# A planner's prices in a two-block network kernel: more fixed time per instruction, half the column price for VectorE's scalar products

## The chip, the cores and the metric

The kernel is one program on one core of a Trainium2 chip. Its time is device time in microseconds (us) from launch to end; three runs stand at 4161.4, 4173.2 and 4182.5, and the median, 4173.2 us, is the time before. Lower is better. Engines are named as the profile names them: PE (TensorE's matmuls), PEld (its weight loads), DVE (VectorE), ACT (ScalarE), POOL (GpSimd), SP (SyncE, which issues most DMAs).

## What is computed

The reference is a float32 network of two blocks over 512 latent and 256 context tokens with 1024 features. The first block normalises, projects, runs three branches (a pooled mixer, a differential attention and a two-way recurrence), merges them and adds a mixture of 32 experts. The second has two layers: long convolutions and a gated recurrence (mLSTM) side by side, then latent attention, each with a convolutional feed-forward. What matters here, cut:

```python
def wkv_step(S, inp):                       # the first block's recurrence, per token
    r, w, k, v, a, b = inp
    sa = jnp.einsum('dbhvk,dbhk->dbhv', S, a)
    S = S * w[..., None, :] + sa[..., None] * b[..., None, :] + v[..., None] * k[..., None, :]
    return S, jnp.einsum('dbhvk,dbhk->dbhv', S, r)

def first_block(x, c, ctx, ...):
    mod = (s_lat @ w_ada[l] + b_ada[l]).reshape(B, N_MOD, 1, D)
    p_l = modulate(x, norm1_g[l], mod[:, 0], mod[:, 1]) @ w_in[l]
    ...                                     # att_l: attention; rwo_l: the recurrence
    mix_l = merge_branches((pool_mixer(pool_l, ...), att_l, rwo_l), gate_l, w_br[l], w_out[l])
    x = x + mod[:, 2] * mix_l
    x = x + mod[:, 5] * hier_moe(f_l, *moe_par)

def second_block(x, c, ctx, ...):           # for both layers
    sh1, sc1, g1, sh2, sc2, g2 = ada_mod(c[:, None, :], ada_w[layer], ada_b[layer])
    x_lat = x_lat + g1 * y_lat              # hyena_mlstm_mixer, then mla_mixer
    x_lat = x_lat + g2 * conv_ffn(...)
    return rmsnorm(x_lat, final_norm)
```

## The kernel before

Matrices are split into two parts, high (`h`) and low (`l`), and multiplied in three passes; the split is a copy on ACT and a subtraction on DVE. Three stretches of the program are woven from streams. Each stream is a Python generator that emits instructions and yields the moment at which its next matmuls could start. `weave` takes in turns the stream of the lowest rank that PE need not wait for.

- **First weave** (57 to 738 us of the profiled execution): inputs of the recurrence (`rwkv_inputs`, weights `ww`), attention (`wa`, then `S`, `P`, `pt`), the pooled mixer and the gates (`wo`, `wg`; the only stream of rank 2), and `rwkv_blocks`, which inverts blocks row by row on DVE (`blt`, `inv`). For each of four pairs of heads, the matmuls `dg` give `blk`, which is transposed to `blkT`; 31 dependent pairs of `blt` and `inv` instructions and two transposes `blkO` follow. The last head's chain ends the weave.
- **Recurrence** (738 to 1310 us): 24 units (`rwkv_unit`: `tkp`, `m`, `pg`, `pT`, `pZ`, `pR`, `pf`) and 24 steps (`rwkv_step`: `pc`, `pw`, `py`), with two units under way and at most three ready. A unit ends with `Zl`. Beside them, at rank 2, 160 matmuls `ada` (modulations of later layers), which depend on weights from memory alone and fill what the others leave.
- **First layer of the second block** (about 2222 to 2860 us): projections (`gp<-h,wi`), the mLSTM's heads (`mw`, `mN`, `mtp`), then long convolutions (`hf`, `fk`, `gtp`, `gc`, `hy`), and 82 further `ada` at rank 2.

What "could start" and "need not wait" mean is decided by `Clock`, a rough account kept while the program is traced. Each instruction is priced at `FIXED[engine] + EACH[engine] * columns`, and placed on its engine's list at the first time at which its inputs are written and there is room; 150 ns (`HOP`) are added from engine to engine. No time of the account is in the program: its only product is the order in which the streams' instructions are emitted. `ready` and `used` hold when tiles are written and free, and `after`, `room` and `later` read them. With nothing ready, the stream that is ready first is taken. When few columns were emitted lately (`active() < LOW`), rank 2 goes first.

The built program's order on each engine follows this one closely, though the build moves single instructions past each other. The rows of order below are the built program's. All instructions that are counted in the account are issued by one helper, so the profile shows them under one line, 350; groups are told apart by tiles.

The merge, the experts, both feed-forwards and the latent attention are each emitted as a single stream.

Of the kernel before, what the change touches and what calls it, by code (L numbers as in the profile page):

```python
# [22 lines left out]
FT = mybir.dt.float32  # L23
# [7 lines left out]
NL, NCX = 512, 256          # latent and context tokens  # L31
NT = NL + NCX               # context first, then latent
NE, CAP = 32, 64            # experts, slots of an expert
NOV = 16                    # further blocks of CAP slots, for experts with more tokens
# [3 lines left out]
ORDER = [[0, 1, 2, 3, 4, 5], [1, 0, 5, 4, 3, 2]]       # tiles of 128 tokens, forwards and backwards  # L38
# [3 lines left out]
# ------------------------------------------------------------------ layouts of the inputs  # L42
def _cols(v):
    """A vector over features as columns of 128 partitions."""
    v = np.asarray(v).reshape(-1)
    return v.reshape(-1, 128).T


def _unit(W, tiles):
    """Columns (128 at a time) of W, as one unit [128, k, n]."""  # L50
    K = W.shape[0]
    w = np.concatenate([W[:, t * 128:(t + 1) * 128] for t in tiles], axis=1)
    return w.reshape(K // 128, 128, -1).transpose(1, 0, 2).reshape(-1)
# [52 lines left out]
# ------------------------------------------------------------------ constants of the shapes  # L106
def _constants():
# [6 lines left out]
    st = [(p[:, None] < p[None, :]) * 1.0, (p[:, None] > p[None, :]) * 1.0]       # [s, t]  # L114
# [3 lines left out]
    for i in range(5, 7):  # L118
        m = 1 << i
        odd = (p // m) % 2 == 1  # L120
        low = ((p[:, None] // m == p[None, :] // m + 1) & odd[:, None]) * 1.0     # [t, s]
        C[f"lv{i}"] = np.concatenate([low, low.T], axis=1)
# [4 lines left out]
    # rotary halves: row d of the product is -u2 or u1  # L127
# [10 lines left out]
    for d in range(2):  # L138
        C[f"neg{d}"] = (1.0 - inc[d]) * -1e30                                     # [s, t]
# [20 lines left out]
def _tables():  # L160
    """More constants of the shapes, read when they are used."""
# [33 lines left out]
def _layout(I):  # L195
    """What the program reads: relaid inputs, and constants of the shapes."""
# [17 lines left out]
    # experts: gate and up in halves of their rows, down in halves of its columns  # L214
# [38 lines left out]
class Clock:  # L253
    """A rough account of when each engine is free and each tile is written, kept while the
    program is traced: it orders streams of instructions that share the engines."""
    FIXED = dict(vector=65.0, scalar=100.0, gpsimd=120.0)
    EACH = dict(vector=1.04, scalar=0.83, gpsimd=2.2)
    HOP = 150.0                 # from one engine to the next
# [7 lines left out]
    def __call__(self, eng, op, a, k):  # L266
# [13 lines left out]
        else:  # L280
            each = self.EACH[eng]
            if eng == "gpsimd" and op in ("tensor_scalar", "memset"):
# [18 lines left out]
    def place(self, eng, t, cost):  # L301
        """The first time from t on at which the engine has room for it."""
# [20 lines left out]
    def place_pe(self, t, cost):  # L323
        """The tensor engine's clock is halved after a tick of too few columns."""
# [8 lines left out]
    def active(self):  # L333
        """Columns of the last tick's length."""
# [29 lines left out]
class Ring:  # L364
    """A pool whose tiles' buffers are accounted for."""
# [13 lines left out]
class Feed:  # L379
    """Weights of a stream, in order: read ahead, and split one part ahead."""  # L380
# [32 lines left out]
class Builder:  # L413
# [7 lines left out]
    # ---- small helpers  # L421
# [25 lines left out]
    def split(self, hi, lo, src):  # L447
        """src as two parts that fp32r carries exactly."""
# [3 lines left out]
    # ---- weights: one unit read and split  # L452
# [13 lines left out]
    def gemm_fm(self, HL, m, kc, segs, tag="g", first=True, last=True, outs=None):  # L466
        """Feature-major product for the m-th 128 columns of a unit: one psum tile per segment.
        segs: (hi, lo, t0, t1), hi and lo [128, kc, tokens]."""
# [7 lines left out]
    def gemm_k(self, outs, H, L, k, segs, a, z, k0=0):  # L476
        """One tile of the contraction, in three passes; k0: where the weights' first tile stands."""
# [7 lines left out]
    # ---- 1/sqrt of a small tile, by Newton's steps  # L485
# [13 lines left out]
    def bcast_cols(self, out, cols, ident=None):  # L499
        """out[:, j*128:...] = cols[:, j] as a row on every partition; cols [128, j]."""  # L500
# [4 lines left out]
    def rms_rows(self, chunks, T, D, pool, tag="s"):  # L505
        """1/sqrt(mean of squares + eps) over all features of feature-major chunks, on every
        partition: a psum tile [128, T]."""
# [25 lines left out]
    # ---- norms of the residuals: the squares follow the sums closely  # L533
    def residual(self):
        """The residual of the latent tokens, and room for its norms."""
# [4 lines left out]
    def square(self, x, n):  # L540
        """The n-th features of a residual have their final values."""
# [10 lines left out]
    def rows(self, Ts, tag="g"):  # L552
        """1/sqrt(mean of squares + eps) of residuals, on every partition: psum tiles."""
# [17 lines left out]
    def modulated(self, norm, l, lo, hi, low, parts, pool, tag="g"):  # L571
        """rmsnorm(x) * (g * (1 + scale)) + shift of residuals, in two parts, into [:, k, t0:t0+T].
        parts: (residual, t0)."""
# [14 lines left out]
    def into(out, steps):  # L588
        """Steps, and their result into a list."""
# [3 lines left out]
    def run(steps):  # L593
        """A stream on its own."""
# [6 lines left out]
    def inner_norm(self, xs, T, g, hi, lo, t0, pool):  # L601
        """rmsnorm(x) * g, in two parts, into [:, k, t0:t0+T]."""
# [6 lines left out]
    # ------------------------------------------------------------------ the program  # L609
    def build(self, stages=("mix", "moe", "l0", "l1")):  # L610
# [21 lines left out]
        if "mix" in stages:             # not before the recurrence's own loads  # L632
# [62 lines left out]
    def gain(self, g, scale, name):  # L695
        """g * (1 + scale), as columns."""
# [4 lines left out]
    # ------------------------------------------------------------------ first block, mixer  # L701
# [2201 lines left out]
```

## Time and profile before

| | us |
|---|---|
| median of three runs | 4173.2 |
| span of the profiled execution | 4168.2 |
| PE busy in it | 3767.0 (90%) |
| DVE busy | 2573.4 (62%) |
| ACT busy | 1679.6 (40%) |
| first weave, 57 to 738 us | 681 |
| recurrence, 738 to 1310 us | 572 |
| first layer of block two, 2222 to 2860 us | 638 |

Read first how busy each engine is in each of the three stretches, and the granted clock of TensorE there (1 is 2.4 GHz, 0.5 is 1.2 GHz). A busy PE includes overlapped starts of matmuls, and time at the lower clock. Then look inside: who waits for whom, and where the filler `ada` stands.

### The profile page before, as it was taken

How to read it: one execution, taken by the hardware profiler on the slowest of the kernel's cores; microseconds unless marked ns; L12 is line 12 of the kernel's file. 1: busy time of each engine (PE TensorE's matmuls, PEld its weight loads, DVE VectorE, ACT ScalarE, POOL GpSimd, SP SyncE). 2: the span in 40 equal slices, each digit the busy share in tenths (PEclk: the TensorE clock that was granted, in tenths of full speed). 3: DMA queues.
4: the chain of work that ended last, by engine and by line, in shares of the span. 5: the costliest groups of instructions: out<-in, count | busy, mean ns of one | idle time of the engine just before them, and what ended most of it. 6: DMA issues, size and time to landing. Idle time of an engine off the chain costs nothing.

```text
span 4168.2 us, 52257 instructions
## 1 busy us (share of the span) xinstructions
PE 3767.0 (90%) x18404; PEld 2830.7 (68%) x18404; DVE 2573.4 (62%) x4611; ACT 1679.6 (40%) x2869; POOL 987.3 (24%) x1066
## 2 busy tenths in 40 slices
PE   8988998799997977888888999898999998999998
PEld 4776665466565755555554887577888886667886
DVE  4587989576665488899984466545333325545444
ACT  3322443333332366666663454223322324434342
POOL 0222211322220367777770000010100100000010
PEclk9989998899987989999999999999999999999999
DMA  4223323534325478888874232421221221012332
GB/s 186 92 75 124 110 70 106 157 121 147 116 80 176 129 246 290 294 298 289 294 242 153 96 124 98 151 74 46 66 64 58 68 64 50 14 40 72 101 96 86
DMA packets 240124, 537.95 MB, mean 129 GB/s; under 512 B 44274, under 2 KB 66451, under 8 KB 237940
## 3 DMA queue, kind: packets, MB, share of 16 engines
q1 hardware_dynamic: 199312, 461.64, 33.4%
q10 hardware_dynamic: 36708, 61.39, 4.2%
q0 software_dynamic: 3840, 11.54, 0.9%
q8 instruction: 148, 2.42, 0.2%
q14 instruction: 116, 0.95, 0.1%
HBM read 486.24 MB, written 48.24 MB: 128 GB/s over the span
## 4 chain that ended last, share of the span: by engine, by line
PE 51%; DVE 9%; DMA 6%; POOL 5%; issue 4%; ACT 3%; SPq 0%; another core or an unknown queue 0%; POOLq 0%; ACTq 0%; DVEq 0%
PE gp L350 32%; DMA ew<-w_exp 3%; POOL el L350 3%; PE ada L350 3%; DVE el L350 2%; PE S L350 2%; PE vp L350 1%; PE eg L350 1%; PE o L350 1%; ACT eh L350 1%; PE fk L350 1%; PE ed L350 1%; PE m L350 1%; PE pc L350 1%; DMA wada<-ada_w 1%
## 5 line engine op out<-in xcount | busy, mean ns | idle before, releaser
L350 POOL TENSOR_TENSOR el<-ew,eh 128x256 fp32r<-128x256 f32 (+1 forms) x384 | 479.7, 1271 | 196.7 <-ACT eh L350 188.8
L350 DVE TENSOR_TENSOR el<-ew,eh 128x768 fp32r<-128x768 f32 x379 | 458.0, 1234 | 58.9 <-ACT eh L350 57.8
L350 ACT CAST wh<-wr 128x512 fp32r<-128x512 f32 (+5 forms) x306 | 199.5, 675 | 600.7 <-PE gp L350 554.1
L350 PE MATMUL gp<-h_hi,wh 128*128 128x512 f32 (+1 forms) x1128 | 401.5, 359 | 6.6 <-ACT h_hi L350 3.8
L350 ACT CAST eh<-ew 128x1024 fp32r<-128x1024 f32 x384 | 381.2, 1048 | 16.4 <-PE ec L350 9.8
L350 PE MATMUL gp<-h_lo,wh 128*128 128x512 f32 (+1 forms) x1128 | 386.1, 357 | 0.7 <-DVE h_lo L350 0.3
L350 DVE TENSOR_TENSOR wl<-wr,wh 128x512 fp32r<-128x512 f32 (+5 forms) x306 | 228.1, 764 | 245.9 <-ACT wh L350 243.7
L350 PE MATMUL gp<-h_hi,wl 128*128 128x512 f32 (+1 forms) x1128 | 343.3, 356 | 0.0
L350 PE MATMUL ada<-wada,adas 128*24 128x512 f32 (+2 forms) x576 | 298.3, 641 | 20.7 <-DMA wada<-w_ada_a 9.9
L350 PE MATMUL eg<-el,xg 128*128 128x512 f32 x512 | 233.3, 457 | 90.0 <-POOL el L350 65.8
L350 POOL MEMSET cvb<- 128x1 f32 x170 | 9.6, 98 | 1068.0 <-DVE fg L350 691.4
L350 PEld LDWEIGHTS gp<-h_hi,wh 128*128 128x128 f32 x1128 | 211.9, 189 | 57.8 <-ACT h_hi L350 8.8
L350 PEld LDWEIGHTS gp<-h_lo,wh 128*128 128x128 f32 x1128 | 212.8, 189 | 34.8 <-DVE h_lo L350 3.2
L350 PE MATMUL eg<-eh,xg 128*128 128x512 f32 x512 | 217.0, 427 | 4.6 <-ACT eh L350 4.5
L350 PEld LDWEIGHTS eg<-el,xg 128*128 128x128 f32 x512 | 103.5, 202 | 168.0 <-POOL el L350 117.0
L350 PEld LDWEIGHTS gp<-h_hi,wl 128*128 128x128 f32 x1128 | 189.8, 190 | 16.7 <-DVE wl L350 0.3
L350 PE MATMUL gp<-z_hi,wh 128*128 128x512 f32 (+1 forms) x528 | 187.8, 356 | 0.0
L350 PE MATMUL gp<-z_lo,wh 128*128 128x512 f32 (+1 forms) x528 | 179.2, 354 | 0.0
L350 PE MATMUL gp<-z_hi,wl 128*128 128x512 f32 (+1 forms) x528 | 158.8, 355 | 0.0
L350 PEld LDWEIGHTS ada<-wada,adas 128*24 128x24 f32 (+2 forms) x576 | 47.1, 103 | 148.4 <-issue 114.1
L350 PE MATMUL gp<-h_lo,wih 128*128 128x256 f32 (+1 forms) x384 | 132.3, 345 | 0.0
L350 PE MATMUL gp<-h_hi,wih 128*128 128x256 f32 (+1 forms) x384 | 128.8, 356 | 0.0
(846 smaller groups left out, 9515.4 us busy)
## 6 DMA issues: line engine op xcount, KB each, us to landing
ew<-w_exp SPq DMA_DIRECT2D x384, 512.0 KB, 5.7
wada<-ada_w SPq DMA_DIRECT2D x192, 256.0 KB, 3.0
wr<-ffn_up SPq DMA_DIRECT2D x176, 256.0 KB, 2.7
wada<-w_ada_b SPq DMA_DIRECT2D x64, 256.0 KB, 3.0
wg<-w_in_a SPq DMA_DIRECT2D x48, 256.0 KB, 2.7
wi<-w_in SPq DMA_DIRECT2D x48, 256.0 KB, 2.6
wr<-ffn_dn SPq DMA_DIRECT2D x32, 384.0 KB, 3.1
wr<-ffn_dn SPq DMA_DIRECT2D x32, 320.0 KB, 3.3
```

The source lines that it names most:

```text
L350: return f(*a, **k)
```

## The change

Three prices of `Clock` grow, and one operation's price per column is halved. DVE's fixed price goes from 65 to 155 ns, ACT's from 100 to 180, POOL's from 120 to 200; the prices per column change little, except POOL's (2.2 to 2.6 ns). `tensor_scalar` on DVE (a tensor with one or two scalars, or a scalar per partition) counts half per column, as it did on POOL. The rest of the diff takes out comments and docstrings.

```diff
 class Clock:
...
-    FIXED = dict(vector=65.0, scalar=100.0, gpsimd=120.0)
-    EACH = dict(vector=1.04, scalar=0.83, gpsimd=2.2)
-    HOP = 150.0                 # from one engine to the next
+    FIXED = dict(vector=155.0, scalar=180.0, gpsimd=200.0)
+    EACH = dict(vector=1.05, scalar=0.85, gpsimd=2.6)
+    HOP = 150.0
     DMA = 2600.0
     TICK, ENOUGH = 10240 / 3, 3060
...
             each = self.EACH[eng]
-            if eng == "gpsimd" and op in ("tensor_scalar", "memset"):
+            if eng == "gpsimd" and op in ("tensor_scalar", "memset") or eng == "vector" and op == "tensor_scalar":
                 each /= 2
             cost = self.FIXED[eng] + each * n
```

The order of the built program changes in the three woven stretches alone. The number of matmuls stays 17,097 in all, with the same work in them. What is not the same in number is ACT's loads of its function tables, which the build puts where two neighbouring functions need different ones: 30 before, 26 now; the four fewer are in the first layer of block two.

**Recurrence, PE, in the last of the 24 units.** Before:

```order
L350 MATMUL pg<-TZ,Ah 128x128 x4
L350 MATMUL ada<-wada,adas 24x512 x2
L350 MATMUL pg<-TZ,Ah 128x128 x4
L350 MATMUL pT<-TZ,identr 128x512
L350 MATMUL pT<-G,TZ 128x128 x4
L350 MATMUL ada<-wada,adas 24x512
L350 MATMUL pT<-TZ,identr 128x512
L350 MATMUL pT<-G,TZ 128x128 x4
```

The change:

```order
L350 MATMUL py<-Us,Mh 128x128
L350 MATMUL py<-Us,Ml 128x128
L350 MATMUL pg<-TZ,Ah 128x128 x4
L350 MATMUL pT<-TZ,identr 128x512
L350 MATMUL pT<-G,TZ 128x128 x4
L350 MATMUL pZt<-const_58,T 128x128 x4
```

The same steps of a unit stand without `ada` between them: of the 160, the last now comes before the 19th unit is through, with 857 matmuls of the recurrence behind it, where it came with 32 behind it.

**Long convolutions, PE, between the short ones (256 tokens, `hy`) and the first filter of the long ones (`fk`).** Before:

```order
L350 MATMUL hf<-hw_22971,hh_22973 128x256 x4
L350 MATMUL ada<-wada,adas 24x512 x3
L350 MATMUL hf<-hw_22971,hh_22973 128x256 x2
L350 MATMUL ada<-wada,adas 24x512 x3
L350 MATMUL gtp<-const_58,hg 128x128 x4
L350 MATMUL ada<-wada,adas 24x512 x2
L350 MATMUL fk<-fch,dft5120h 128x256
L350 MATMUL fk<-fch,nyq 128x256
```

The change:

```order
L350 MATMUL hf<-hw_23002,hh_23004 128x256 x5
L350 MATMUL gtp<-const_58,hg 128x128 x4
L350 MATMUL fk<-fch,dft5120h 128x256
L350 MATMUL fk<-fch,nyq 128x256
L350 MATMUL gtp<-const_58,hg 128x128
```

Eight `ada` are gone from this place. Of the stretch's 82, the projections' part held 13 and now holds 22; behind the projections stood 53, now 39; ahead of them 16, now 21.

**First weave, DVE, in the last head's chain of `blt` and `inv`.** Before:

```order
L350 TENSOR_TENSOR blt<-inv,blkT 128x24x24
L350 TENSOR_TENSOR nm<-mx 128x1
L350 TENSOR_TENSOR wgl<-wg,wgh 128x512
L350 TENSOR_REDUCE inv<-blt 128x24
L350 TENSOR_SCALAR nm<-nm 128x1
L350 TENSOR_TENSOR wgl<-wg,wgh 128x512
L350 TENSOR_TENSOR blt<-inv,blkT 128x25x25
```

The change:

```order
L350 TENSOR_TENSOR blt<-inv,blkT 128x22x22
L350 TENSOR_REDUCE inv<-blt 128x22
L350 TENSOR_TENSOR blt<-inv,blkT 128x23x23
L350 TENSOR_REDUCE inv<-blt 128x23
L350 TENSOR_TENSOR blt<-inv,blkT 128x24x24
L350 TENSOR_REDUCE inv<-blt 128x24
L350 TENSOR_TENSOR blt<-inv,blkT 128x25x25
```

The attention's and the gates' instructions stand earlier, so this chain's end is alone. Counted in the built order: between the first and the fourth `blkT`, DVE had 749 instructions and now has 788; from the fourth to the last `blkO`, 111 and now 100. PE had 1428 matmuls between the last `dg` of the first head and that of the fourth, and now has 1565; behind that, to the weave's end, 203 and now 81.

## Rows read from the trace of the kernel before

**Rows 1.** The page's part 1: busy us, share of span, instructions.

```profile
PE 3767.0 (90%) x18404; PEld 2830.7 (68%) x18404; DVE 2573.4 (62%) x4611; ACT 1679.6 (40%) x2869; POOL 987.3 (24%) x1066
```

**Rows 2.** Windows of the three woven stretches: length, busy times, clock, DMA share.

```profile
core 0: us, PE busy (x) PEld busy (x) DVE busy (x) ACT busy (x) POOL busy (x), PEclk, DMA share, GB/s
...
57.00:738.00 681.00, 621.06 (x2800) 457.93 (x2800) 541.76 (x1092) 243.29 (x499) 118.25 (x133) 0.92 0.28 95
738.00:1310.00 572.00, 511.60 (x2927) 344.92 (x2927) 369.53 (x704) 199.67 (x390) 150.96 (x190) 0.89 0.38 116
...
2222.00:2860.00 638.00, 603.33 (x3297) 465.96 (x3296) 338.42 (x872) 233.29 (x462) 36.42 (x112) 0.95 0.32 106
```

**Rows 3.** Groups by form, whole span: busy us, mean ns of one, idle before.

```profile
L350 ACT ACT_TABLE_LOAD x30 | 38.5, 1283 | 8.6 <-DVE mx L350 3.6 <-issue 2.1 <-DVE mu L350 1.3
...
L350 DVE TENSOR_TENSOR G<-pg,const 128x512 fp32r<-128x512 f32 x48 | 32.7, 685 | 16.4 <-PE pg L350 16.2
...
L350 DVE TENSOR_SCALAR P<-P,sm 128x768 f32<-128x768 f32 x32 | 19.8, 618 | 0.7
```

**Rows 4.** Windows of the first weave, from one `blkT` to the next, and after.

```profile
244.00:392.00 148.00, 133.24 (x636) 104.63 (x635) 120.73 (x223) 42.89 (x77) 34.83 (x34) 0.91 0.29 98
392.00:530.00 138.00, 126.15 (x530) 85.73 (x529) 125.33 (x260) 53.03 (x121) 22.32 (x22) 0.94 0.32 106
530.00:670.00 140.00, 125.71 (x533) 84.62 (x531) 125.05 (x268) 54.80 (x125) 21.87 (x23) 0.94 0.30 99
670.00:738.00 68.00, 59.06 (x216) 39.12 (x216) 60.74 (x118) 21.50 (x51) 5.82 (x3) 0.90 0.25 80
```

**Rows 5.** The tile `blkT`: ns min/median/max, first and last start.

```profile
L350 DVE STREAM_TRANSPOSE blkT<-blk x4: 1234/1236/1248, 244.2 to 670.5; 128x1024 f32<-128x1024 f32 x4
```

**Rows 6.** Groups of PE in 57 to 738 us, with idle time before and releasers.

```profile
L350 PE MATMUL gp<-h1l_hi,wgh 128*128 128x512 f32 x192 | 86.2, 449 | 5.3 <-ACT gt L350 5.2
...
L350 PE MATMUL S<-kx,q 64*128 64x384 f32 x128 | 54.9, 543 | 7.6 <-ACT P L350 5.9 <-DMA kx<-at_k 1.6
...
L350 PE MATMUL dg<-AR,BK 64*128 64x128 f32 x96 | 16.8, 348 | 8.8 <-DVE BK L350 6.0 <-DVE blk L350 2.6 <-DVE nm L350 0.2
```

**Rows 7.** Windows of the recurrence; behind 1137 us start its last 853 other matmuls.

```profile
738.00:1137.00 399.00, 360.53 (x2010) 231.46 (x2011) 261.91 (x477) 142.40 (x276) 117.17 (x154) 0.90 0.43 136
1137.00:1310.00 173.00, 151.06 (x919) 113.46 (x918) 107.62 (x227) 57.27 (x114) 33.79 (x36) 0.86 0.24 71
```

**Rows 8.** The same windows, `ada` alone: PE, PEld, ACT (two PE records each matmul).

```profile
738.00:1137.00 399.00, 133.19 (x254) 19.73 (x254) 0.57 (x1) 0.90 0.43 136
1137.00:1310.00 173.00, 37.11 (x66) 5.04 (x66) 0.57 (x1) 0.86 0.24 71
```

**Rows 9.** Start and end of a unit (tiles `tkh`, `Zl`): first and last start.

```profile
L350 ACT CAST tkh<-tkp x24: 576/586/600, 751.9 to 1249.5; 128x512 fp32r<-128x512 f32 x24
...
L350 DVE TENSOR_TENSOR Zl<-Zt,Zh x24: 682/1240/3883, 794.3 to 1282.8; 128x512 fp32r<-128x512 f32 x24
```

**Rows 10.** Timeline of PE in the last unit: start, us, instruction.

```profile
1266.25 0.45 PE L350 MATMUL pT<-TZ,identr 128*128 128x512 f32 x1
1266.54 0.56 PE L350 MATMUL pT<-G,TZ 128*128 128x128 f32 x4
```

**Rows 11.** Windows of the projections, and of the convolutions with `ada` in them.

```profile
2290.00:2590.00 300.00, 297.11 (x1792) 253.93 (x1791) 181.98 (x554) 150.14 (x295) 4.03 (x64) 0.97 0.29 99
...
2685.00:2785.00 100.00, 94.58 (x490) 63.96 (x489) 46.41 (x92) 22.09 (x53) 19.32 (x28) 0.99 0.34 107
```

**Rows 12.** Timeline of PE around `gtp`; in brackets idle time and its releaser.

```profile
2725.89 0.63 PE L350 MATMUL gtp<-const,hg 128*128 128x128 f32 x4 [2.71 <-DMA hg<-hy_x]
2726.44 1.90 PE L350 MATMUL ada<-wada,adas 128*24 128x512 f32 x4
...
2801.51 0.63 PE L350 MATMUL gtp<-const,hg 128*128 128x128 f32 x4 [2.62 <-DMA hg<-hy_g]
2802.81 1.22 PE L350 MATMUL gc<-gt_hi,dft5120h 128*128 128x256 f32 x4 [0.68 <-ACT gt_hi L350]
```

## The prediction, made before the changed kernel was run

> **What bounds the kernel now.** The page's first part comes first: PE is busy for 90% of the span, DVE for 62%, ACT for 40% [rows 1]. That makes PE the engine whose gaps count on the whole, but the change touches three stretches alone, and the share is an average over all. So the windows of the three woven stretches come next [rows 2]. PE stands idle there for 681 − 621 = 60 us, 572 − 512 = 60 us and 638 − 603 = 35 us, at a mean granted clock of 0.92, 0.89 and 0.95. A perfect order could bring back no more than these 155 us and what the clock loses; a worse order can take more.
>
> The first weave is the one in which another engine is nearly as full. From the first `blkT` to the fourth, 426.3 us [rows 5], DVE is busy for 120.7 + 125.3 + 125.1 = 371.1 us (87%) and PE for 385.1 us (90%) [rows 4]. PE's waits in the whole weave that have a name are small and spread: 5.3 us before the gates, 7.6 before `S`, 8.8 before `dg` [rows 6]. DVE's row of dependent instructions is what the weave ends on, so the moment of the fourth `blkT` matters.
>
> In the recurrence a unit takes from its first cast `tkh` (751.9 first, 1249.5 last) to its `Zl` (794.3 first, 1282.8 last): 33.3 us for the last one, while 24 of them take 530.9 us, 22.1 us each [rows 9]. With two under way, 16.7 us each would be the floor of the dependent work. Of the filler, 127 `ada` stand in the first 399 us and 33 in the last 173 us [rows 8]; one costs PE 1.90 / 2 = 0.95 us [rows 12].
>
> In the first layer of block two, the projections fill PE for 297.1 of 300 us and the part of the convolutions that has `ada` for 94.6 of 100 us [rows 11]. That stretch leaves little to win.
>
> The new prices are nearer to what DVE does. A `G` of 512 columns now counts 155 + 1.05 x 512 = 693 ns, 597 before, and takes 685; a scalar product over 768 columns counts 155 + 0.525 x 768 = 558 ns, 864 before, and takes 618 [rows 3]. Better prices do not by themselves make a better order, since the weave only asks who is ready first and takes filler when nobody is. With dearer DVE and ACT instructions the account sees PE wait more often, and rank 2 is taken earlier. All the moves below have that shape: filler and side work come forward, and the ends of the stretches lose it.
>
> **The change part by part.** The account has no instruction in the program, so no matmul is added or removed, and the price is that of moves alone.
>
> *A, first weave.* DVE has 39 instructions more between the first and the fourth `blkT`. At the mean of that part, 371.1 us / 751 = 0.49 us, they are +19 us. Behind the fourth, DVE has 11 fewer, at 60.7 / 118 = 0.51 us each [rows 4]: −6 us, and if the waits in it (68.0 − 60.7 = 7 us) go too, since the chain is then alone, −13 us. With DVE as the pacemaker that is +6 to +13, of which I take +9. The ends: on PE, 137 more matmuls stand ahead of the fourth head's `dg`, mostly gates, at 385.1 us / 1428 = 0.27 us each, +37 us; less the 7 us at the end, +30. Downwards, if the earlier gates fill all the gaps, the 426.3 us shrink to DVE's own 371 + 19 = 390, −36 us, with −13 behind: −49. DVE's row is the nearest, because its 87% includes few waits that an order could cure, and the work that the end loses is work that the middle must do.
>
> *B, recurrence, first part.* 33 more `ada` come ahead: 33 x 0.95 = +31 us. PE's idle time there is 399 − 360.5 = 38.5 us [rows 7], of which the start until the first `tkh`, 14 us [rows 9], has nothing to fill it with. At the best the other 25 us take them: +6. At the worst they stand before ready work: +31. I take the middle, +18.
>
> *B, tail.* The last 857 matmuls, 173 us before, lose 33 `ada`: −31 us of PE. But the filler stood in holes. In the first part `ada` had 133.2 of 399 us (33%), in the tail 37.1 of 173 us (21%) [rows 8]; DVE's busy share was 261.9 / 399 = 66% and 107.6 / 173 = 62% [rows 7]. With a third less filler, the work on the other engines went no faster, so it is not the filler that holds it up. The place shows why: between `pg` and the `pT` that needs `G` now lies a single matmul, 0.29 us from its start to the next (1266.25 to 1266.54) [rows 10], against 685 ns for `G` [rows 3]; the `ada` taken away leave a wait of about their length. At the floor of 16.7 us a unit the tail's 173 / 22.1 = 7.8 units would take 131 us, −42; if every hole stays open, 0. I take −8. Together B is +18 − 8 = +10, with ends of +6 − 42 = −36 and +31.
>
> *C, first layer of block two.* Nine more `ada` in the projections, where PE has no gap [rows 11]: 9 x 0.95 = +9 us. Five more ahead of them: +5, of which about 2 paid. Behind, 14 fewer: −13, of which about 6 come back as waits: a `gtp` that waited 2.71 us with `ada` near it and one that waited 2.62 and left 0.68 more without [rows 12] show that the filler hides two or three us a time, in the two or three places that lose it. Sum: +9 + 2 − 13 + 6 = +4. The four table loads that go, 4 x 1.28 = 5 us of ACT [rows 3], lie on an engine that is busy for 233 of 638 us [rows 2], and I count −1 for them, with ends of 0 and −5. C is +3, with ends of −10 (the nine are hidden, the loads count) and +15 (the filler at the end was all cover).
>
> A rule speaks for C's lower end. PE's busy time says that the projections have 3 us to spare, while its weight loads are busy for 253.9 of 300 us, 85% [rows 11]. The Trainium skill ("Perfetto Trace Analysis", section Identifying the Most-Contended Engine) holds that busy time of matmuls is no good measure of headroom, since pipelined instructions look otherwise in a trace than what they cost, and that the share of weight loads is to be read. By it 46 us would be free in the projections, the nine `ada` would cost nothing there, C would be −6, and the total 4186. No row here shows an `ada` taken in for nothing beside `gp`.
>
> The sum is 9 + 10 + 3 = +22 us. The profiled execution's span is 4168.2 us, and 5.0 us lie around it to the median of 4173.2. So 4168.2 + 22 + 5.0 = 4195.
>
> **The rivals.**
>
> *Faster: the waits in the first weave are cured.* PE's waits behind ACT and DVE there were made by prices that were too low: 65 ns for a start that counts 155 now. If the earlier gates fill PE's 41 us of gaps between the first and the fourth `blkT` without holding up DVE, A is −40 instead of +9, and the rest stays: 4173 − 40 + 13 = 4146. For it speaks that the prices fit [rows 3]; against it, DVE at 87% must do 39 instructions more in that part. It decides if DVE's share there rises to 95%.
>
> *Slower: the recurrence's tail without filler loses the clock.* The granted clock was 0.86 in the tail with 33 `ada` in it, and 0.97 to 0.99 where PE never waited [rows 7, 11]. If half of the tail's remaining 151.1 − 37.1 = 114 us of PE falls to the lower of the two levels (1.2 GHz, a mean of 0.75), they take 114 x 0.86 / 0.75 = 131 us, +17 us in place of −8; with the first part at its upper end, +31, B is +48 and the total 4173 + 9 + 48 + 3 = 4233. Against it: the dependent chains may hide a slower PE. It decides if the granted clock behind the last `ada` is under 0.78.
>
> *Nothing: the change doesn't do what it says.* The same instructions stand on the same engines, the moves are local, and each gain at one end is paid at the other: A, B and C each within 5 us, 4173. For it: every `ada` that comes earlier does go away later. Against it: the tail's row on DVE's share.
>
> **How the numbers follow.** Something like the sum, 4183 to 4215: 0.41. Faster by the first weave, about 4146: 0.19. Slower by the tail, about 4233: 0.18. Nothing: 0.22. The forecast is 4195. The range runs from 4140, which takes in most of the faster case, to 4235, the slower one. A measurement of this kernel can tell about 0.5%, 21 us, from no change, and the sum lies on that edge. Slower by over that are the tail's 0.18 and over half of the forecast's, 0.24; faster the first weave's 0.19, less what falls within 21 us of it, 0.18 in all; the same what is left, 0.40.
>
> **What would show it right or wrong.** In the profile of the changed kernel the fourth `blkT` should start some 19 us later than 670.5 and the weave end some 9 us later than 738; the last `ada` of the recurrence should start before 1180, and the recurrence be 582 us long, with its last 165 us at DVE's old share and a clock below 0.86; the layer should be 641 us long, with the projections 9 us longer. A is wrong if the fourth `blkT` starts no later than before: then DVE was not the pacemaker. B's tail is wrong if its units come at less than 20 us each: then the filler did hold up the chains. C is wrong if the projections grow by less than 4 us with nine more `ada` in them. Any difference over 5 us outside the three stretches would mean that something but the order has changed.

## The result and the profile after

The changed kernel takes 4198.6 us in the median of 11 runs, against 4173.2 before: a ratio of 1.0066 with a 95% interval of 1.005 to 1.0081, slower by 25 us. The forecast was 4195. Its profiled execution has a span of 4196.4 us, 28.2 more than that of before.

The page's first part and the windows of the three stretches, moved to where they now lie (length, busy times, clock, DMA share; they answer to [rows 1] and [rows 2]):

```profile
PE 3780.8 (90%) x18404; PEld 2855.7 (68%) x18404; DVE 2571.2 (61%) x4611; ACT 1673.6 (40%) x2865; POOL 987.3 (24%) x1066
```

```profile
57.00:749.00 692.00, 613.70 (x2808) 453.51 (x2808) 544.16 (x1104) 244.34 (x500) 117.25 (x134) 0.93 0.28 94
749.00:1333.00 584.00, 533.46 (x2919) 374.65 (x2919) 366.07 (x692) 198.53 (x390) 152.34 (x189) 0.85 0.37 113
2250.00:2888.00 638.00, 599.77 (x3296) 464.21 (x3295) 338.34 (x870) 227.44 (x457) 36.31 (x112) 0.96 0.33 106
```

The first weave is 11 us longer, the recurrence 12, the layer the same; PE's busy time in the recurrence rose by 22 us at a clock of 0.85 instead of 0.89. To place it closer, these landmarks of both traces serve (start times in us):

| | before | after | difference |
|---|---|---|---|
| first weave, to the last `blkO` | 735.7 | 746.1 | +10.4 |
| recurrence, from there to the last `py` | 561.3 | 573.9 | +12.6 |
| merge and experts, to the last `cp` | 910.5 | 914.9 | +4.4 |
| first layer, to the last `hy` | 622.2 | 622.9 | +0.7 |
| the rest of the span | 1338.5 | 1338.5 | 0.0 |

The +4.4 lies where the two programs have the same order. In ten further kernels with that order this stretch takes 914 to 921 us, so the execution of before was a short one there. The three woven stretches account for +23.7.

**First weave.** From one `blkT` to the next and behind the last (as [rows 4]), the tile's own line (as [rows 5]) and PE's waits (as [rows 6]):

```profile
238.00:391.00 153.00, 140.18 (x695) 110.38 (x694) 124.83 (x238) 45.80 (x80) 31.45 (x31) 0.96 0.31 104
391.00:529.50 138.50, 130.38 (x563) 89.94 (x561) 128.63 (x274) 58.22 (x135) 24.68 (x26) 0.98 0.34 113
529.50:693.00 163.50, 145.82 (x596) 99.73 (x596) 132.44 (x279) 60.47 (x138) 23.11 (x23) 0.92 0.28 91
693.00:749.00 56.00, 25.04 (x86) 14.78 (x85) 50.83 (x102) 9.37 (x24) 2.46 (x3) 0.72 0.15 44
```

```profile
L350 DVE STREAM_TRANSPOSE blkT<-blk x4: 1235/1245/1246, 237.9 to 693.0; 128x1024 f32<-128x1024 f32 x4
```

```profile
L350 PE MATMUL gp<-h1l_hi,wgh 128*128 128x512 f32 x192 | 83.8, 436 | 0.3 <-ACT gt L350 0.2
...
L350 PE MATMUL S<-kx,q 64*128 64x384 f32 x128 | 52.0, 524 | 1.5 <-PE gp L350 0.5 <-ACT P L350 0.5 <-ACT pr L350 0.2
...
L350 PE MATMUL dg<-AR,BK 64*128 64x128 f32 x96 | 16.6, 343 | 8.6 <-DVE nm L350 4.7 <-DVE rsq_w L350 2.2 <-DVE blk L350 1.0
```

The fourth `blkT` starts at 693.0, 22.5 us later, and the stretch behind it is 12 us shorter, with DVE busy for 50.8 of 56 us and PE for 25.0 where it had 59.1. The named waits before the gates and `S` have gone from 5.3 and 7.6 us to 0.3 and 1.5, which won no time.

**Recurrence.** Its first part and its last 173 us (as [rows 7]; the last `ada` starts at 1150), with `ada` alone behind them (PE, PEld, ACT, as [rows 8]):

```profile
749.00:1150.00 401.00, 372.41 (x2047) 224.58 (x2047) 253.86 (x452) 140.82 (x274) 114.67 (x149) 0.96 0.49 153
1150.00:1323.00 173.00, 156.88 (x854) 146.27 (x853) 108.50 (x226) 56.30 (x114) 35.15 (x38) 0.63 0.08 24
```

```profile
749.00:1150.00 401.00, 159.36 (x320) 25.16 (x320) 0.58 (x1) 0.96 0.49 153
1150.00:1323.00 173.00, 0.41 (x1) 0.00 (x0) 0.57 (x1) 0.63 0.08 24
```

Without a single `ada` the last 173 us are as full as before, PE 156.9 against 151.1 us. The granted clock is 0.63 in place of 0.86, so most of the tail runs at the lower of the two levels, 1.2 GHz. The first part has all the filler and a clock of 0.96 in place of 0.90. DVE's work per us stayed: 108.5 of 173 us, 107.6 before.

**First layer.** The projections by their first matmul group (duration min/median/max in ns, first and last start), before and after; then the windows that answer to [rows 11]:

```profile
L350 PE MATMUL gp<-h_hi,wih x384: 274/390/795, 2293.6 to 2590.2; 128*128 128x256 f32 x192
```

```profile
L350 PE MATMUL gp<-h_hi,wih x384: 274/390/748, 2320.5 to 2622.3; 128*128 128x256 f32 x192
```

```profile
2318.00:2618.00 300.00, 297.39 (x1775) 247.78 (x1774) 175.36 (x522) 142.48 (x286) 4.06 (x64) 0.98 0.32 104
2716.00:2816.00 100.00, 87.49 (x491) 67.70 (x491) 51.12 (x105) 23.18 (x57) 21.65 (x30) 0.92 0.23 70
```

From the first to the last start of this group the projections take 301.8 us instead of 296.6, +5. The part ahead of them is 0.5 us shorter and the part behind 3.9, where PE is busy for 87.5 of 100 us, without `ada`, at a clock of 0.92 (94.6 at 0.99 before).

### The profile page after: what moved, and what is told of

Its sections match the earlier page's. It is cut to its first block, busy times and chain, and to the rows that moved or that the text cites. A ratio compares the mean times of both kernels' runs of the same rounds, so it can differ in the third digit from the quotient of the medians.

```text
span 4196.4 us, 52227 instructions
## 1 busy us (share of the span) xinstructions
PE 3780.8 (90%) x18404; PEld 2855.7 (68%) x18404; DVE 2571.2 (61%) x4611; ACT 1673.6 (40%) x2865; POOL 987.3 (24%) x1066
## 3 DMA queue, kind: packets, MB, share of 16 engines
q1 hardware_dynamic: 199312, 461.64, 33.3%
## 4 chain that ended last, share of the span: by engine, by line
PE 52%; DVE 8%; DMA 5%; POOL 5%; issue 5%; ACT 3%; SPq 0%; another core or an unknown queue 0%; POOLq 0%; ACTq 0%; DVEq 0%
PE gp L350 32%; POOL el L350 4%; PE ada L350 3%; DMA ew<-w_exp 3%; DVE el L350 2%; PE S L350 2%; PE eg L350 1%; PE vp L350 1%; PE o L350 1%; PE pc L350 1%; PE fk L350 1%; ACT eh L350 1%; PE m L350 1%; PE py L350 1%; PE ed L350 1%
## 5 line engine op out<-in xcount | busy, mean ns | idle before, releaser
L350 ACT CAST eh<-ew 128x1024 fp32r<-128x1024 f32 x384 | 381.1, 1048 | 16.3 <-PE ec L350 9.7
L350 PE MATMUL ada<-wada,adas 128*24 128x512 f32 (+2 forms) x576 | 284.9, 619 | 31.5 <-DMA wada<-ada_w 10.5
```

The lines of the kernel that those rows point to most:

```text
L350: return f(*a, **k)
```

## The experiments

Two questions were open: whether each stretch pays for its own new order, and by what; and whether the prices make the loss, or the one order that they happen to draw. All runs are collected here; the experiments follow. "To the tail" runs from the last `blkO` to the start of the 840th matmul, counted back from the last `py`, that is neither filler nor a transpose of its results (`adc`), "tail" from there to the start of the last `py`, "filler" counts `ada` (or the dummies below) in the tail, and "layer" is the first layer from the last `cp` to the last `hy`. Medians are in us, of 10 to 12 executions each (6 for the dummies, 4 for the new prices + 3 ns and for the last row); ratios are against the kernel before, with their intervals. The other columns come from one profiled execution each.

| kernel | weave | to the tail | tail | filler | layer | median | ratio |
|---|---|---|---|---|---|---|---|
| before | 735.7 | 394.4 | 166.9 | 38 | 622.2 | 4173.2 | |
| the change | 746.1 | 404.8 | 169.2 | 0 | 622.9 | 4198.6 | 1.0066 (1.005 to 1.0081) |
| new prices in the weave | 748.3 | 382.0 | 169.2 | 31 | 615.5 | 4172.7 | 1.0002 (0.9988 to 1.0016) |
| in the recurrence | 733.6 | 398.8 | 174.2 | 0 | 614.5 | 4177.7 | 1.0011 (0.9993 to 1.0029) |
| in the layer | 733.4 | 396.6 | 166.5 | 38 | 624.4 | 4180.1 | 1.0013 (1.0 to 1.0026) |
| dummies in the tail | 748.4 | 408.1 | 164.4 | 33 | 621.1 | 4206.9 | 1.0079 (1.0056 to 1.0102) |
| gates held | 756.9 | 388.9 | 164.1 | 11 | 624.8 | 4192.8 | 1.0043 (1.0027 to 1.0058) |
| new prices + 3 ns | 746.6 | 423.4 | 168.0 | 10 | 622.8 | 4215.6 | 1.0092 (1.0069 to 1.0116) |
| new prices − 3 ns | 736.9 | 401.5 | 159.2 | 7 | 621.3 | 4178.7 | 1.0011 (0.9995 to 1.0026) |
| old prices + 3 ns | 721.0 | 391.4 | 173.8 | 48 | 616.3 | 4161.8 | 0.9971 (0.995 to 0.9992) |
| old prices − 3 ns | 739.2 | 390.8 | 158.0 | 39 | 616.2 | 4161.4 | 0.9965 (0.9944 to 0.9985) |
| fixed prices alone | 727.6 | 433.5 | 169.1 | 3 | 621.2 | 4206.8 | 1.0067 (1.0049 to 1.0085) |
| halved price alone | 706.5 | 447.9 | 164.1 | 45 | 611.7 | 4184.7 | 1.0014 (0.9997 to 1.0031) |
| `ada` from the layer | 724.7 | 398.1 | 174.2 | 51 | 607.7 | 4151.1 | 0.9927 (0.9901 to 0.9952) |

In the rows of the fixed and the halved price alone, 48 and 161 matmuls of the weave fall behind the last `blkO`, so that their weave is short and the next column long; weave and "to the tail" are read together there, 1161 and 1154 us against 1130 before. In the old prices − 3 ns and in the halved price alone, 12 and 3 more `ada` stand behind the last `py`.

**Each stretch alone.** The account switches its prices where a stretch ends, so that the order of the others is that of before, or close to it.

```diff
+    def prices(self, new):
+        self.FIXED, self.EACH = (NEW_FIXED, NEW_EACH) if new else (Clock.FIXED, Clock.EACH)
+        self.HALF = new
...
         self.clock = Clock()
+        self.clock.prices(True)       # first weave; False for the other two
...
                     self.weave(*zip(self.RANKS, ...))
+                    self.clock.prices(False)      # recurrence: True in the second kernel
...
             self.rwkv(e)
+            self.clock.prices(False)      # layer: True in the third kernel
```

The first weave:

> The new prices hold from the program's start to the end of the first weave, the old ones from there on, so PE's order in the first weave is word for word that of the change, and in the recurrence it is another one, with filler to its end as before (134 matmuls behind the last ada). Theory that the stretches add up (the last transposed block 10 us later, as in the changed kernel): 4173 + 10 = 4183, with 5 us either way for the recurrence's order. Rival that the first weave's lateness is made up in the recurrence, which waits for its inputs: 4173.

Measured: 4172.7, no loss. The weave did end late, at 748.3, 12.6 us behind that of before, but the recurrence took 551.2 us, 10 less than before. It has an order of its own, since the account enters it from another first weave. The gain lies in its first part, 382.0 us against 394.4. Little of it is a shorter wait for inputs, as the rival has it: the first `tkh` starts 13.6 us behind the last `blkO` where it started 16.3 behind, 2.7 us of the 10. The weave's loss itself repeats: three traces with the order of before end at 733.4 to 735.7, three with that of the change at 746.1 to 748.4. That another order of the recurrence, by the same prices, made it up by chance is the reading that is left; no run isolates it.

The recurrence:

> The new prices hold in the recurrence alone (860 matmuls behind the last ada, 97% of the order as in the change). Theory that the tail without filler costs the clock: the recurrence is 12 to 15 us longer, 4173 + 13 = 4186, with a granted clock under 0.7 behind the last ada and over 0.94 before it. Rival that the loss came from the first weave's order alone: 4173.

Measured: the recurrence is 573.0 us, 11.7 longer, as in the change, with a clock of 0.97 ahead of the last `ada` and 0.60 behind it, 4.4 us of it in the first part and 7.3 in the tail. The change, of whose order 97% is the same, had 10.4 and 2.3, so one execution can't place the loss within the recurrence. The median rose by 4.5 us with an interval of −3 to +12, which doesn't settle the size.

The layer:

> The new prices hold from the recurrence's end on, which changes the order in the first layer of block two alone. Theory: 6 us more in the projections, 8 less behind them, and 3 between, 4174. Rival, by weight loads, that the ada in the projections are free: 4167.

Measured: 4180.1, +7 (0 to +11). The traces bear it out in a larger set: in the seven kernels with the new or nearly new order of that layer it takes 621.1 to 624.8 us, mean 622.6; with the order of before it takes 622.2, 615.5 and 614.5, and 616.2 and 616.3 with nearly that order, mean 616.9. The one profiled execution of before was the longest of its kind, and hid a loss of about 6 us. By parts, in the means of the same seven and five: 1 us more ahead of the projections, 7 more in them (301.5 against 294.4; 300.9 to 301.9 against 291.8 to 296.8), 3 less behind. So the rival of free filler in the projections is wrong, and the 14 `ada` taken from behind them were nearly free there. By their medians the three kernels lose 11 us together, where the change lost 25: in the first of them the recurrence is 10 us shorter by another order, so the parts don't simply add.

**Dummies in the tail.** Work is added where the filler went away:

```diff
+        def filler(n):
+            yield from self.ada_steps(wp, self.ada_jobs())
...
+            for _ in range(n):                    # n = 33
+                yield 0.0
+                self.mm(p, z, W)                  # 24x512, zeros; read by nobody
...
-        self.weave(*gens, (2, self.ada_steps(...)))
+        self.weave(*gens, (2, filler(33)))
```

> The change, with 33 more matmuls of the shape of ada behind the last ada of the recurrence at the filler's rank, on zeros, whose result nobody reads: work that is added. Theory that the tail's time is the granted clock's: the clock there goes from 0.62 back to 0.8 or more, the tail gets 7 to 10 us shorter though PE has 31 us more to do, 4198 - 8 = 4190. Rival that the dependent chains set the tail: nothing is won, and up to 31 us are lost, 4198 to 4230.

Windows of the recurrence's two parts, and of the dummies alone in the same windows (PE, PEld):

```profile
751.00:1155.00 404.00, 377.83 (x2045) 227.59 (x2046) 252.03 (x451) 140.14 (x273) 114.60 (x149) 0.94 0.49 152
1155.00:1321.00 166.00, 150.99 (x922) 117.88 (x920) 107.00 (x219) 57.06 (x116) 35.11 (x38) 0.86 0.08 25
```

```profile
1155.00:1321.00 166.00, 31.21 (x66) 5.49 (x66) 0.86 0.08 25
```

The clock is back at 0.86, and with 31 us of useless work the tail is 4.8 us shorter than in the change (164.4 against 169.2). The matmuls that count took 151.0 − 31.2 = 120 us there, where they took 157 in the change. So the clock took what the missing filler had freed on PE: that part of the theory is shown. It is not shown that the clock is worth a net gain: the whole was 4206.9, in the rival's range and not 4190, with an interval that overlaps that of the change; the recurrence as a whole took 572.5 us against 573.9.

**Gates held.** Gates came forward in the first weave, so the last six wait for the fourth head:

```diff
-        for b, n in at:
+        for j, (b, n) in enumerate(at):
+            while j >= 18 and self.heads_in < 4:     # counted up where a head's blocks are emitted
+                yield self.later()
```

> The change, with the last six of the 24 gates of the first weave held until the fourth head's blocks are emitted (before, 17 gates had started by the fourth head's last dg; with the change 22). Theory that the gates that came forward hold up the fourth head: its blkT comes at 670 to 676 again instead of 693, the weave ends at 736 to 739 instead of 746 to 748, and the whole is 4198 - 9 = 4189. Rival that something else of the new order makes the head late: blkT stays at 690 to 695, 4198.

Measured: 4192.8, with an interval that overlaps that of the change; the fourth `blkT` still starts at 692.2, and the weave ends later yet, at 756.9, with gates now at its end. That is the rival's number, but the hold was weaker than meant: by the starts of `gt`, 20 gates were through ahead of the fourth `blkT`, where it was 22 with the change and 18 before, so only two were moved. The run doesn't clear the gates; it shows 7 us less work for PE ahead of that `blkT` and a stretch 3 us shorter. What the length goes with shows in the stretch from the first to the fourth `blkT` of six kernels: before, the change, gates held, new prices + 3 and − 3 ns, old prices + 3 ns (length, then busy times of PE, PEld and DVE):

```profile
244.20:670.50 426.30, 384.90 (x1694) 274.83 (x1692) 371.41 (x751) 150.53 (x322) 79.02 (x79) 0.93 0.30 101
```

```profile
237.90:693.00 455.10, 416.48 (x1852) 300.11 (x1852) 385.97 (x789) 164.49 (x351) 79.24 (x80) 0.95 0.30 102
```

```profile
240.00:692.20 452.20, 409.18 (x1785) 291.84 (x1784) 379.52 (x777) 158.85 (x339) 78.28 (x79) 0.92 0.30 100
```

```profile
237.60:692.90 455.30, 414.82 (x1850) 298.44 (x1850) 386.13 (x790) 163.80 (x350) 79.70 (x80) 0.95 0.31 102
```

```profile
231.50:674.00 442.50, 397.46 (x1709) 285.08 (x1708) 374.99 (x759) 151.64 (x321) 82.01 (x79) 0.90 0.29 97
```

```profile
243.20:659.70 416.50, 379.89 (x1622) 269.09 (x1621) 363.40 (x749) 147.82 (x317) 73.50 (x77) 0.91 0.30 99
```

PE's idle time is 41.4, 38.6, 43.0, 40.5, 45.0 and 36.6 us, much the same in stretches of 416 to 455 us; DVE's is 54.9, 69.1, 72.7, 69.2, 67.5 and 53.1. Over all fourteen kernels PE's lies between 36 and 46 us in stretches of 402 to 456. The length follows PE's work. Both engines get more to do in most of these orders, but one tells them apart: with the new prices − 3 ns DVE has 3.6 us more to do than before, PE 12.6, and the stretch is 16.2 us longer. No run moved the work of one engine alone, so this is a fit over orders, not an experiment on one cause.

**Prices shifted by 3 ns.** The rival theory of the whole result was that the account draws one order out of many. It is tried with prices that no one could call other prices:

```diff
-    FIXED = dict(vector=155.0, scalar=180.0, gpsimd=200.0)
+    FIXED = dict(vector=158.0, scalar=183.0, gpsimd=203.0)    # and 152, 177, 197
...
-    FIXED = dict(vector=65.0, scalar=100.0, gpsimd=120.0)     # before
+    FIXED = dict(vector=68.0, scalar=103.0, gpsimd=123.0)     # and 62, 97, 117
```

> The change with each of the three fixed prices 3 ns higher (158, 183, 203). Theory that the loss comes with the higher prices: a weave that ends at 745 to 749, a recurrence of 570 to 576 us and 4193 to 4203 in all. Rival that each set of prices draws one order out of many of different worth: the recurrence lies anywhere in 551 to 575, the whole in 4165 to 4205.

> The change with each of the three fixed prices 3 ns lower (152, 177, 197). As for prices up: 745 to 749, 570 to 576 and 4193 to 4203 by the theory that higher prices cost; anywhere in 551 to 575 and 4165 to 4205 by the rival that the order is drawn by accident.

> The kernel before with each of its three fixed prices 3 ns higher (68, 103, 123), which still gives filler to the recurrence's end (64 matmuls behind the last ada). By the theory that the new prices cost: a weave that ends at 733 to 738, a recurrence of 558 to 564 us, 4168 to 4178. By the rival of accident: 730 to 750, 551 to 575, 4160 to 4200.

> The kernel before with each of its three fixed prices 3 ns lower (62, 97, 117). 96.7% of the first weave's order is that of before; filler runs over the recurrence's end (14 ada behind it). Theory that the lower prices are the better ones: 4165 to 4178, a weave of 733 to 738. Rival of accident: 4160 to 4215, the weave anywhere in 720 to 757 even with so little of the order changed.

Measured: 4215.6 and 4178.7 around the change's 4198.6, 4161.8 and 4161.4 beside the 4173.2 of before. Three ns, a fiftieth of the smallest new price, move the whole by −20 or +17 us, as much as the change did. The rival is right on the spread, which is even wider than it said: the new prices + 3 ns lie above its 4205, with a recurrence of 591.4 us where it ended at 575, and the old prices + 3 ns have a weave of 721.0 where it began at 730. The first theory missed all but one of the sums and stretches that it named (the weave of 746.6). Something is left for the first theory: all three with the new prices lie above all three with the old, with means of 4197.6 and 4165.5. Three draws each make that likely, not sure.

Two tails far apart in clock, with no filler (the recurrence alone) and with 39 `ada` (old prices − 3 ns):

```profile
1132.00:1307.00 175.00, 162.50 (x853) 151.11 (x852) 106.61 (x219) 56.71 (x115) 34.56 (x38) 0.60 0.08 24
```

```profile
1128.00:1288.00 160.00, 149.50 (x929) 106.05 (x928) 108.75 (x212) 57.22 (x115) 32.41 (x38) 0.95 0.29 89
```

PE is busy for 93% of either, DVE for about 107 us of either. Over all fourteen kernels the tail takes 158 to 174 us whatever is in it: 167.1 in the mean of the eight with 31 to 51 filler matmuls, at granted clocks of 0.85 to 0.96, and 167.3 in the mean of the six with 0 to 11, at 0.60 to 0.75.

**The two parts of the change.** The first kernel keeps the new prices and undoes the halving, the second has the halving alone:

```diff
     FIXED = dict(vector=155.0, scalar=180.0, gpsimd=200.0)
-            if eng == "gpsimd" and op in ("tensor_scalar", "memset") or eng == "vector" and op == "tensor_scalar":
+            if eng == "gpsimd" and op in ("tensor_scalar", "memset"):       # first kernel
...
     FIXED = dict(vector=65.0, scalar=100.0, gpsimd=120.0)
-            if eng == "gpsimd" and op in ("tensor_scalar", "memset"):
+            if eng == "gpsimd" and op in ("tensor_scalar", "memset") or eng == "vector" and op == "tensor_scalar":   # second
```

> The change without the halved price of DVE's scalar products. 768 matmuls of the recurrence stand behind the last ada (857 in the change), 15 before. Theory that filler taken early is paid: the recurrence 570 to 580 us, and 4190 to 4205 in all. Rival that the orders are worth what they happen to be, whatever became of the filler: recurrence 550 to 592, weave 720 to 757, 4160 to 4215. Either way the recurrence's last 840 matmuls take 159 to 174 us.

> The prices of before with the halved price of DVE's scalar products alone. Filler runs to the recurrence's end and 5 ada over it. Theory that filler taken early is what is paid: recurrence 555 to 566 us, 4165 to 4180. Rival of accident: recurrence 550 to 592, weave 720 to 757, 4160 to 4215.

Measured: 4206.8 and 4184.7. The fixed prices alone bring the filler forward, and lose as much as the whole change, 2 us more than the theory's range; the tail's 169.1 us are in the range named for either case. The halved price leaves filler to the recurrence's end and was to lose nothing; it lies 11 us over before, outside the theory's range and inside the rival's, though its ratio's interval still holds 1, and its trace is 21.5 us late by the last `py` (706.5 + 612.0 against 735.7 + 561.3). Both recurrences, 602.6 and 612.0 us, lie beyond either range, in part because matmuls of the weave fall into them. Filler isn't all, then.

**`ada` from the layer into the recurrence.** If the tail takes filler for nothing, more of it can go there (with the switch of prices at the recurrence as above, not shown again):

```diff
-        return [(self.D["w_ada_b"], ...), (self.D["ada_w0"], ...)]
+        return [(self.D["w_ada_b"], ...), (self.D["ada_w0"], ...),
+                (self.D["ada_w1"][:, :, :3072], self.s2, *(t[:, :24] for t in self.mod2[1]))]
...
-            ada = self.ada_steps(..., [(D["ada_w1"], self.s2, *self.mod2[1])])
+            ada = self.ada_steps(..., [(D["ada_w1"][:, :, 3072:], self.s2, *(t[:, 24:] for t in self.mod2[1]))])
```

> The prices of before plus 3 ns, with the change's prices in the recurrence alone, and 48 of the 96 ada of the first layer of block two put behind the recurrence's 160 (its filler then goes on to 94 matmuls from its end). Theory that the tail of the recurrence takes filler for nothing: weave 721, recurrence 565 to 580, and the layer shorter by 48 x 0.95 = 46 us less the cover that it loses, 25 to 40 us: 4120 to 4155. Rival that the tail pays for them: recurrence 600 or more, no gain, 4165 to 4185.

The `ada` alone in the recurrence's first part and tail (PE, PEld, ACT):

```profile
725.00:1123.00 398.00, 156.42 (x314) 24.34 (x314) 0.57 (x1) 0.98 0.51 158
1123.00:1297.00 174.00, 50.26 (x102) 7.46 (x102) 1.15 (x2) 0.90 0.30 94
```

Measured: 4151.1, 0.9927 (0.9901 to 0.9952), the fastest of all and ahead of both kernels; against the old prices + 3 ns, from which it starts, it is 11 us faster by the medians, with intervals that just touch. The recurrence took 572.2 us as expected, with 50 us of `ada` in a tail of 174. But the layer lost only 8.6 us against the kernel with the same weave's prices (616.3 to 607.7), not 25 to 40: its part behind the projections went from 237.3 to 228.0 us for 48 `ada`, 46 us of PE, fewer. Filler was nearly free there too. The execution that was profiled is the longest of its four (4165.6 us), and the recurrence is 7 us longer in it than with the old prices + 3 ns, so the traces don't show where the gain of the median comes from.

## Why the prediction was right, point by point

**The total and the three sums held.** 4195 was forecast with 4140 to 4235, and the measured 4198.6 is slower by 0.66% by the ratio, the direction with the largest chance (0.42, against 0.40 for the same). A was +9 and is +10.4, B was +10 and is +12.6, C was +3 and is +0.7 in the two profiled executions, about +6 over the kernels with either order. Repeats of the two orders of the first weave put A nearer to +13. Most of the signs that were named came: a fourth `blkT` some 19 us later (22.5), a weave 9 us longer (10), the last `ada` before 1180 (1150), a recurrence of 582 us (584 in the windows) with its tail under a clock of 0.86. The layer of 641 us did not show in these two traces (638), nor the 9 us in the projections (5).

**A had the right sum by the wrong pacemaker.** The 39 instructions more on DVE are there (751 and 789), but cost 14.6 us, not 19, and DVE's idle time rose by 14 as well. What grew with the stretch is PE: 31.6 us more work with 41.4 and 38.6 us of idle time, and the other orders give the same. The step that failed is the choice of DVE's row as the nearest; PE's, which the prediction made the upper end at +30 (+37 less 7), was the right one. Two things made up for it: the first `blkT` came 6.3 us earlier, and the end gave back 12.1 us, the more hopeful of the two values for it. −6.3 + 28.8 − 12.1 = +10.4. The sign that was named for A, a fourth `blkT` later than before, came, but it would have come with either engine as the pacemaker, so it couldn't find this out.

**B had the right sum from two terms that were both off.** The first part was to cost +18 and cost 10.4: the filler added 26.2 us of PE there [rows 8], while the clock rose from 0.90 to 0.96. Over the kernels, the five with at most 129 `ada` ahead of the tail take 391 us in the mean and the seven with 149 to 160 take 403 (the two whose weave reaches into it left out), so about a third of the filler's price is paid there, with a scatter of up to 20 us. The tail was to gain 8 and lost 2. The step that failed is that it was priced at the clock of before: the rows showed 0.86 with filler in it, the prediction kept that for its forecast, and the slower clock stood in a rival. The rival's condition was met, 0.63 where it decided from 0.78, and the same matmuls took 157 us of PE instead of 114. But its price of +17 was too high as well, since the 37 us of filler that were gone left room for nearly all of it. That the work on the other engines doesn't go faster without filler was right, and holds from 0 to 51 filler matmuls. The units' own time stayed too: from `tkh` to `Zl` the last eight took 37.9 us in the mean before and 37.8 after. The floor of 16.7 us a unit, by which the tail could have gained 42, came from the last unit alone (33.3 us); with the mean of all 24, 37.1 us, it would be 18.6.

**C's parts were right in sign, and one was too large.** In the two traces: ahead of the projections −0.5 (+2 forecast), in them +5 (+9), behind −4 (−7). In the means over the kernels: +1, +7 and −3. The term that was mis-sized is the one behind: 14 `ada` fewer were to win 7 us net and won 3, about a fifth of their price, and 48 fewer won 9 in the last experiment, again a fifth. The rule of the Trainium skill that was set against it (its page "Perfetto Trace Analysis", section Identifying the Most-Contended Engine) would have had the nine `ada` free. That page names the share of peak work (MFU) beside the share of weight loads, and the prediction read the second alone. The runs don't agree with that reading: by the means the projections grew by 7 of the 8.6 us that nine cost, with weight loads busy for 253.9 and 247.8 of 300 us before and after. Of the 96 `ada` of that layer the text ahead of the prediction counts 82, as 14 stand in front of the place from which it counted. The differences that the forecast used (five more ahead, nine more in the projections, 14 fewer behind) are the same either way.

**The rivals.** The waits cured: the waits went as it said (5.3 and 7.6 to 0.3 and 1.5) and it won nothing, as PE had 31.6 us more to do ahead of the fourth head. DVE's share there, which was to rise to 95% for it, fell from 87% to 85%. The change doing nothing: not so, but a neighbour of it at 3 ns less did (1.0011).

**What the right number hides.** The largest flaw, which no rival of the prediction had, is that it treated the order as a consequence of the prices that can be summed, when it is also one draw out of many. Neighbours of the same prices took 4179 and 4216, so the sum could have been right in all its reasons and 20 us off, and that it came within 4 us is partly luck. It was built on counts in the very order that was to run, which is why it could be near at all. What stays open: why the recurrence's first part takes 389 to 423 us with 149 to 160 `ada` in it; whether the tail would be shorter without filler at the full clock, as no run has both; and whether honest prices are worse in themselves, which the six draws suggest and don't show.

## What to carry to other kernels

Before a gain or loss is credited to a planner's new prices, shift them by a few per cent (2 to 5% here) and time the neighbours: that alone moved the time by 11 to 20 us, and found orders 12 us better than that of before. Find the pacemaker of a stretch by what stays constant when its length changes (PE's 36 to 46 us of idle time over fourteen orders), not by the row of waits that looks nearest in one trace. Filler taken away from the recurrence's tail won nothing: it kept its length while the clock fell. That dependent chains set it is the likeliest reading, not one that a run isolates. Before movable work is taken out of a stretch like it, price it there by runs; in this tail it cost next to nothing.

## What the runs showed of the hardware that was not expected

PE looked equally full with and without filler: 93% busy at a granted clock of 0.60 with none, and 93% at 0.95 with 39 matmuls of it. 33 matmuls on zeros raised the clock of a tail from 0.63 to 0.86 and took 31 us of PE without making it longer. And in kernels whose order is the same there, the merge and the experts took from 914 to 921 us from one execution to the next, the 910.5 of before being the shortest.
